# The closing part of a decoder block: gathered block, norm weight and last sums rearranged, with VectorE in program order

## The chip, the cores and the metric

The kernel runs on one core of a Trainium2 chip. The metric is the time of one execution on the device in microseconds (us). Three runs of the kernel before took 1557.12, 1559.18 and 1560.58 us; the median is 1559.18 us. In the rows PE is the matrix engine (PEld its weight loads), DVE the vector engine, ACT the scalar engine, POOL GpSimd, and SP the engine whose queue issues most transfers; a q behind a name (DVEq, SPq) is that engine's sequencer.

## What is computed

The reference is one decoder block over 512 tokens of width 1024: attention and gated linear attention side by side, then a channel mixer that retrieves experts, then a final norm. Only the mixer's end and the norm bear on the change:

```
def peer_ffn(h, wq, subkeys, u, v):      # per token: 8 heads x 16 of 16384 experts
    ...
    ub = jnp.take(u, eb, axis=0)
    hid = jax.nn.gelu(jnp.einsum('tkd,td->tk', ub, xb), approximate=False) * gb
    vb = jnp.take(v, eb, axis=0)
    return jnp.einsum('tk,tkd->td', hid, vb)

x = x + gate2 * peer_ffn(...)            # gate2: one row of 1024 for the sequence
y = x * rsqrt(mean(x * x) + 1e-6) * final_norm_w
```

The last two lines are the closing part: for each token the mixer's sum times gate2, plus the residual x, the norm over 1024 columns, and the product with the norm's weight.

## The kernel before

The 512 tokens are four blocks of 128. For three of them (DENSE, blocks 0 to 2, 384 tokens) the mixer isn't gathered: all 16,384 experts are run through as 128 chunks of 128. For chunk c, `u_part(c)` makes the hidden values (`ph`, 24 matmuls of 128x384) and `v_part(c)` scales them by the gates and splits them and the chunk's rows of v into a high and a low part (`Ah`, `Al`, `vc..h`, `vc..l`; the low parts are DVE's, lines 60 and 1029). `v_matmuls` adds the chunk's contribution to six PSUM accumulators `acc0` to `acc5` (block i, column half q: `acc[2*i+q]`): 3 matmuls of 128x512 (`mm3`, lines 64 to 66) for each accumulator, 18 for a chunk. The last four chunks (LAST = 4, c = 124 to 127) are held back and done block by block, first half 0, then half 1, so that block 0 is ready first.

The fourth block (GB = 3) is gathered. POOL issues 128 gathers of u rows (`gu`, line 887) and 128 of v rows (`gv`, line 897) into a ring of buffers; DVE multiplies each `gu` with `h2n` and sums it (line 889) and adds each `gv` to `gacc` (line 902). `gather_to`, line 1068, spreads them over 124 chunks.

At c = 112 the tile `h2n` is overwritten with gate2: DVE makes a diagonal tile `dg` (line 1074), PE multiplies it with ones (`g2b`, line 1079), ACT copies the result to `h2n` (line 1080). From there on `h2n` is the gate row.

`finish(n, ...)`, lines 1039 to 1059, closes a block: load x (line 1043), gate (1047), add x (1048), squares on ACT with a sum for each half (1049), their sum (1050), `rstd_of` (lines 70 to 82: mean, Ln and Exp on ACT, one Newton step on DVE in lines 78 to 81), then one instruction for each half that multiplies with the rstd and with the norm weight `fwb` (1058), and the store (1059). For block 1 the scale is ACT's (1055) and the weight POOL's (1056). Block 3 is finished ahead of the last four chunks' preparation, then blocks 0, 1, 2 as their accumulators end.

The order on each engine comes from a scheduler that simulates the program, except for POOL, which keeps the order of the code. On an engine the instructions start in their order; a waiting one holds back those behind it.

Of the kernel before, what the change touches and what calls it, by code (L numbers as in the profile page):

```python
# [17 lines left out]
P = 128  # L18
D = 1024
# [3 lines left out]
EPS = 1e-6  # L23
# [13 lines left out]
GR = 5  # L37
# [4 lines left out]
def peer_block_kernel(ctx: ExitStack, tc: tile.TileContext, a: dict, out: bass.AP):  # L42
    nc = tc.nc
# [3 lines left out]
    ps = ctx.enter_context(tc.tile_pool(name="ps", bufs=2, space=PSUM, side="left"))  # L47
# [60 lines left out]
    x1d = dr.tile([NT, P, D], F32, name="x1d")  # L108
# [14 lines left out]
    def pbank(name):  # L123
        return ps.tile([P, 512], F32, tag="ph", name=name)
# [46 lines left out]
    xf = frA.tile([P, 2, 32], F32, name="xf")  # L171
# [5 lines left out]
    for L in LW:  # L177
        m = 64 >> L
# [50 lines left out]
    for n in range(NT):  # L229
        sq = frA.tile([P, D], F32, tag="m4", bufs=2, name=f"sqa{n}")  # L230
        ss = frA.tile([P, 2], F32, tag="ss", bufs=2, name=f"ssa{n}")
# [3 lines left out]
        r = rstd_of(frA, ss[:, 0:1], float(D), 1, f"ra{n}")  # L235
# [376 lines left out]
    h2n = h2p.tile([P, D], F32, name="h2n")  # L612
# [74 lines left out]
    def u_part(c, lo_eng=None):  # L687

        j = c // 2 % 2
        if j == 0:  # L690
            u_part.raw[c % 2] = raw([P, 2, KD, P], f"u{c}")
            nc.sync.dma_start(u_part.raw[c % 2], a["uT"][c // 4 + (c % 2) * (P // 4)])
        uh, ul = hilo(u_part.raw[c % 2][:, j], [P, KD, P], f"uc{c}", lo_eng or nc.vector)
        ph = ps.tile([P, 512], F32, tag="ph", name=f"ph{c}")[:, :TD]
        for k in range(KD):
            mm3(ph, uh[:, k, :], ul[:, k, :], h2Th[:, k, :TD], h2Tl[:, k, :TD], k == 0, k == KD - 1)
        ge = dnA.tile([P, NGRP, TG], F32, tag="ge", bufs=RING, name=f"ge{c}")
        gef = ge.rearrange("p g t -> p (g t)")
# [226 lines left out]
    gp = ctx.enter_context(tc.tile_pool(name="gp", bufs=1, side="left", reuse_waits="tile"))  # L925
# [106 lines left out]
    def v_matmuls(parts, blocks=range(len(DENSE)), qs=(0, 1)):  # L1032
        for c, Ah, Al, vh, vl in parts:
            for i in blocks:
                for q in qs:
                    mm3(acc[2 * i + q], Ah[:, i * P:(i + 1) * P], Al[:, i * P:(i + 1) * P],
                        vh[:, q * 512:(q + 1) * 512], vl[:, q * 512:(q + 1) * 512], c == 0, c == P - 1)

    def finish(n, srcs, xr=None, pool=False):
        gate2b = h2n  # L1040
        y = gp.tile([P, D], F32, tag="gr", bufs=GR, name=f"y{n}")
        xr = xr if xr is not None else gp.tile([P, D], F32, tag="gr", bufs=GR, name=f"xf{n}")
        nc.sync.dma_start(xr, x1d[n])
        ss = dn.tile([P, 2], F32, tag="ss", bufs=2, name=f"ssf{n}")
        for q in range(2):
            qs = slice(q * 512, (q + 1) * 512)
            nc.vector.tensor_tensor(y[:, qs], srcs[q], gate2b[:, qs], OP.mult)
            nc.vector.tensor_tensor(y[:, qs], y[:, qs], xr[:, qs], OP.add)
            nc.scalar.activation(xr[:, qs], y[:, qs], AF.Square, accum_out=ss[:, q:q + 1])
        nc.vector.tensor_tensor(ss[:, 0:1], ss[:, 0:1], ss[:, 1:2], OP.add)  # L1050
        r = rstd_of(dn, ss[:, 0:1], float(D), 1, f"rf{n}")
        for q in range(2):
            qs = slice(q * 512, (q + 1) * 512)
            if pool:
                nc.scalar.activation(y[:, qs], y[:, qs], AF.Copy, scale=r)
                nc.gpsimd.tensor_tensor(y[:, qs], y[:, qs], fwb[:, qs], OP.mult)
            else:
                nc.vector.scalar_tensor_tensor(y[:, qs], y[:, qs], r, fwb[:, qs], op0=OP.mult, op1=OP.mult)
            nc.sync.dma_start(out[n * P:(n + 1) * P, qs], y[:, qs])

    LEAD = 8
    for c in range(1, 1 + LEAD, 2):
# [22 lines left out]
    for i in range(len(DENSE)):  # L1085
# [62 lines left out]
```

## Time and profile before

| | us |
|---|---|
| median of three runs | 1559.18 |
| the profiled execution | 1555.13 |
| its span, first to last instruction | 1553.4 |
| PE busy / share of the span | 1493.2 / 96% |
| DVE busy | 1251.8 / 81% |
| ACT busy | 688.8 / 44% |
| POOL busy | 412.9 / 27% |
| TensorE clock granted, mean | 0.99 of full speed |

The profiled execution is 1.7 us longer than its span, and 4.05 us shorter than the median. Busy shares are means over the whole span, and the closing part is its last 2%: there the stretch itself has to be read.

### The profile page before, as it was taken

Reading aid. Unit: us, or ns where it says so; the run is one execution under the profiler, and the core shown is the slowest. Engines: PE = TensorE matmul, PEld = TensorE weight load, DVE = VectorE, ACT = ScalarE, POOL = GpSimd, SP = SyncE. Lnnn points to the kernel's source line nnn. Section 1 sums busy time; section 2 is a strip of 40 time slices with the busy share of each in tenths; the row PEclk is TensorE's granted clock in tenths of the full one; section 3 lists DMA queues with packets and bytes.
Section 4 is the critical chain, followed back from the end, with each engine's and each line's share of the span. In section 5 each row is a group of like instructions: output and inputs, shape, how many; then the busy total and the mean of one; then the engine's idle time right before and its main releaser. Section 6 shows DMA issues by size and latency. Waiting matters only on the chain.

```text
span 1553.4 us, 24408 instructions
## 1 busy us (share of the span) xinstructions
PE 1493.2 (96%) x9379; PEld 1328.2 (86%) x9379; DVE 1251.8 (81%) x2476; ACT 688.8 (44%) x1078; POOL 412.9 (27%) x327
## 2 busy tenths in 40 slices
PE   4999989899999999999999999999999999999996
PEld 3787878888998999999888888888888888888885
DVE  7578668589989898995678778878888878887997
ACT  5545576433445666564333333333333333333343
POOL 1000000144500000003243334433434434434550
PEclk9999999999999999999999999999999999999998
DMA  9253444262346677679998999888998989898893
GB/s 349 89 204 131 171 142 173 108 239 92 127 155 188 198 239 235 201 239 388 380 348 317 339 348 346 322 340 333 364 330 329 338 340 354 326 340 334 292 331 129
DMA packets 154932, 409.67 MB, mean 264 GB/s; under 512 B 10288, under 2 KB 77120, under 8 KB 142400
## 3 DMA queue, kind: packets, MB, share of 16 engines
q1 hardware_dynamic: 108736, 261.30, 47.2%
q0 software_dynamic: 36864, 134.23, 23.0%
q10 hardware_dynamic: 9216, 12.59, 2.2%
q8 instruction: 73, 1.20, 0.3%
q14 instruction: 43, 0.35, 0.1%
HBM read 366.14 MB, written 41.94 MB: 263 GB/s over the span
## 4 chain that ended last, share of the span: by engine, by line
PE 63%; DVE 3%; DMA 2%; ACT 1%; issue 1%; DVEq 0%; ACTq 0%; SPq 0%
PE acc L65 11%; PE acc L64 11%; PE acc L66 11%; PE ph L66 8%; PE ph L64 8%; PE ph L65 8%; PE pg L874 4%; DMA Gd<-gs 1%; DMA gr<-Gd 1%; DVE o L867 1%; ACT gs L876 0%; DVE o L862 0%; DVE oh L819 0%; DVE oh L822 0%; DVE oh L817 0%
## 5 line engine op out<-in xcount | busy, mean ns | idle before, releaser
L887 POOL DMA_INDIRECT gu<-in_u_dram,ix_u x128 | 170.2, 1329 | 531.5 <-PE pg L874 273.5
L897 POOL DMA_INDIRECT gv<-in_vP_dram,ix_v x128 | 171.0, 1336 | 214.9 <-DVE gu L889 183.1
L902 DVE SCALAR_TENSOR_TENSOR gacc<-gv,hg,gacc 128x1024 f32<-128x1024 f32 x127 | 162.7, 1281 | 3.3 <-DMA gv<-in_vP_dram,ix_v 3.1
L889 DVE SCALAR_TENSOR_TENSOR gu<-gu,h2n 128x1024 f32<-128x1024 f32 x128 | 156.0, 1219 | 5.9 <-DMA gu<-in_u_dram,ix_u 5.9
L1028 ACT ACTIVATE Ah<-ge 128x384 fp32r<-128x384 f32 x64 | 33.6, 525 | 155.1 <-PE acc L65 155.1
L1028 ACT ACTIVATE Ah<-gel 128x384 fp32r<-128x384 f32 x64 | 33.6, 525 | 154.4 <-PE acc L65 154.4
L876 ACT ACTIVATE gs<-pg 128x512 f32<-128x512 f32 x96 | 94.3, 1108 | 9.8 <-PE pg L874 9.8
L867 DVE TENSOR_TENSOR o<-o,gp 128x1024 bf16<-128x1024 bf16 x144 | 91.0, 687 | 4.3
L874 PE MATMUL pg<-o,o 128*128 128x128 bf16 x1152 | 79.3, 223 | 5.3 <-DVE o L867 5.3
L874 PEld LDWEIGHTS <-o 128*128 128x128 bf16 x1152 | 69.7, 99 | 14.4 <-issue 8.5
L953 POOL IOTA iot<- 128x256 bf16 x1 | 1.5, 1541 | 282.8 <-DVE h2Tl L675 282.8
L1029 DVE TENSOR_TENSOR Al<-gel,Ah 128x384 fp32r<-128x384 f32 x64 | 35.6, 556 | 45.2 <-ACT Ah L1028 45.2
L699 ACT ACTIVATE ge<-ph 128x384 f32<-128x384 f32 x128 | 60.8, 475 | 23.8 <-PE ph L66 23.7
L862 DVE TENSOR_TENSOR o<-iot,t 128x2048 bf16<-128x2048 bf16 x48 | 58.5, 1218 | 4.9 <-ACT t L842 4.9
L1029 DVE TENSOR_TENSOR Al<-ge,Ah 128x384 fp32r<-128x384 f32 x64 | 35.5, 555 | 19.2 <-ACT Ah L1028 18.1
L1024 DVE TENSOR_TENSOR ge<-ge,gr 128x384 f32<-128x384 f32 x64 | 35.4, 553 | 10.9 <-ACT ge L699 10.9
L212 DVE SCALAR_TENSOR_TENSOR macc<-wa,scs,macc 128x1024 f32<-128x1024 f32 x28 | 39.0, 1392 | 4.9 <-DMA wa<-in_w_ada_dram 4.7
L1024 DVE TENSOR_TENSOR gel<-gel,gr 128x384 f32<-128x384 f32 x64 | 32.8, 553 | 0.0
L65 PE MATMUL pq<-h2Tl,wq_0h 128*128 128x512 f32 (+1 forms) x80 | 27.9, 349 | 1.2 <-DVE h2Tl L675 1.2
L64 PE MATMUL pq<-h2Th,wq_0h 128*128 128x512 f32 (+1 forms) x80 | 28.0, 352 | 1.0 <-ACT qha L751 1.0
L65 PE MATMUL pq<-h2Tl,wq_1h 128*128 128x512 f32 (+1 forms) x80 | 28.2, 353 | 0.0
L66 PE MATMUL pq<-h2Th,wq_1l 128*128 128x512 f32 (+1 forms) x80 | 28.2, 352 | 0.0
(2599 smaller groups left out, 5077.1 us busy)
## 6 DMA issues: line engine op xcount, KB each, us to landing
u<-in_uT_dram SPq DMA_DIRECT2D x64, 1024.0 KB
v<-in_vP_dram SPq DMA_DIRECT2D x64, 1024.0 KB
Gd<-gs SPq DMA_DIRECT2D x24, 1024.0 KB
gr<-Gd SPq DMA_DIRECT2D x16, 1536.0 KB
wa<-in_w_ada_dram SPq DMA_DIRECT2D x20, 1024.0 KB
gsp<-ge ACTq DMA_DIRECT2D x64, 192.0 KB
gel<-gsp SPq DMA_DIRECT2D x32, 384.0 KB
wi<-in_w_in_dram SPq DMA_DIRECT2D x9, 1024.0 KB
```

Source lines behind the costliest of these rows:

```text
L64: nc.tensor.matmul(acc, lh, rh, start=start, stop=False)
L65: nc.tensor.matmul(acc, lh, rl, start=False, stop=False)
L66: nc.tensor.matmul(acc, ll, rh, start=False, stop=stop)
L867: nc.vector.tensor_tensor(o2[:, :, m], o12[:, :, 1], gp3[:, g0:g0 + H, m, None].to_broadcast([P, H, P, 2]), OP.mult)
L874: nc.tensor.matmul(pt[:, i, :], o12[:, g, 0, :, r], o2[:, g, m, :, r], start=(m == 0), stop=(m == 2))
L876: nc.scalar.activation(gs[:, :, t0 + 4 * f:t0 + 4 * f + 4].rearrange("p b a -> p a b"), pt, AF.Copy)
L887: nc.gpsimd.indirect_dma_start(out=ur, out_offset=None, in_=a["u"], in_offset=bass.IndirectOffsetOnAxis(ap=ix_u[:, s:s + 1], axis=0))
L889: nc.vector.scalar_tensor_tensor(ur, ur, 1.0, h2n, op0=OP.mult, op1=OP.mult, accum_out=hid[:, s:s + 1])
L897: nc.gpsimd.indirect_dma_start(out=vr, out_offset=None, in_=a["vP"], in_offset=bass.IndirectOffsetOnAxis(ap=ix_v[:, s:s + 1], axis=0))
L902: nc.vector.scalar_tensor_tensor(gacc, vr, hg[:, s:s + 1], gacc, op0=OP.mult, op1=OP.add)
L1024: nc.vector.tensor_tensor(ge, ge, v_part.g[:, :, c % CG, :], OP.mult)
L1029: nc.vector.tensor_tensor(Al, gef, Ah, OP.subtract)
```

## The change

It rewrites `finish`. Block 3 gets a function of its own, `finish_gathered`, called after chunk 122: whole rows of 1024 columns, squares and mean in one DVE instruction, and the inverse root by DVE alone (`rsqrt_dve`: an integer start value and three Newton steps of three instructions). The gathers are spread over 122 chunks instead of 124. Blocks 0 to 2 use a class `Finish`: gate and add (`gated`), squares on ACT (`squared`), the product with the norm weight as DVE instructions of their own (`weighed`), which stand beside ACT's Ln and Exp, then the Newton step, and the final scale by ACT or DVE (`close`). Block 2's half 1 is closed before the last four chunks: `acc5` ends at chunk 123 and is gated and added at once, and the last four chunks' part of it goes to two new accumulators of 256 columns, `pl512` and `pl768`. Its output leaves in three pieces of 320, 384 and 320 columns. From `fs = [...]` on DVE keeps the order of the code.

```diff
                 for q in qs:
+                    end = P - LAST if (i, q) == (len(DENSE) - 1, 1) else P
                     mm3(acc[2 * i + q], ..., c == 0, c == end - 1)
-    def finish(n, srcs, xr=None, pool=False):
...
+    def rsqrt_dve(pool, m, name):
+        nc.vector.tensor_scalar(y.bitcast(I32), m.bitcast(I32), -0.5, 1597463007.0, op0=OP.mult, op1=OP.add)
+        for _ in range(3):
+            nc.vector.scalar_tensor_tensor(t, y, y, m, op0=OP.mult, op1=OP.mult)
+            nc.vector.tensor_scalar(t, t, -0.5, 1.5, op0=OP.mult, op1=OP.add)
+            nc.vector.tensor_tensor(y, y, t, OP.mult)
+    def finish_gathered():
+        nc.sync.dma_start(xr, x1d[GB])
+        nc.vector.tensor_tensor(y, gacc, h2n, OP.mult)
+        nc.vector.tensor_tensor(y, y, xr, OP.add)
+        nc.vector.scalar_tensor_tensor(xr, y, 1.0 / D, y, op0=OP.mult, op1=OP.mult, accum_out=ss)
+        nc.vector.tensor_scalar(ss, ss, EPS, None, op0=OP.add)
+        r = rsqrt_dve(dn, ss, "r3")
+        nc.vector.scalar_tensor_tensor(y, y, r, fwb, op0=OP.mult, op1=OP.mult)
+        nc.sync.dma_start(out[GB * P:(GB + 1) * P, :], y)
+    class Finish:
+        def gated(self, cs, src):
+            nc.vector.tensor_tensor(self.y[:, cs], src, h2n[:, cs], OP.mult)
+            nc.vector.tensor_tensor(self.y[:, cs], self.y[:, cs], self.xr[:, cs], OP.add)
+        def squared(self, cs):
+            nc.scalar.activation(xr[:, cs], y[:, cs], AF.Square, scale=1.0 / 32.0, accum_out=self.ss[:, j:j + 1])
+            if j == 1:
+                nc.vector.tensor_scalar(self.ss[:, 3:4], self.ss[:, 0:1], self.ss[:, 1:2], EPS, op0=OP.add, op1=OP.add)
+        def weighed(self, *css):
+                nc.vector.tensor_tensor(self.y[:, cs], self.y[:, cs], fwb[:, cs], OP.mult)
+        def close(self, rest, parts):
+            if len(self.ps) == 3:
+                nc.vector.tensor_tensor(m, m, ss[:, 2:3], OP.add)
+            nc.scalar.activation(r, m, AF.Ln)
+            nc.scalar.activation(r, r, AF.Exp, scale=-0.5)
+            self.weighed(*rest)
+            nc.vector.scalar_tensor_tensor(t, r, r, m, op0=OP.mult, op1=OP.mult)
+            nc.vector.tensor_scalar(t, t, -0.5, 1.5, op0=OP.mult, op1=OP.add)
+            nc.vector.tensor_tensor(r, r, t, OP.mult)
+            for on_act, cs in parts:
+                if on_act:
+                    nc.scalar.activation(y[:, cs], y[:, cs], AF.Copy, scale=r)
+                else:
+                    nc.vector.tensor_scalar(y[:, cs], y[:, cs], r, None, op0=OP.mult)
+                nc.sync.dma_start(out[n * P:(n + 1) * P, cs], y[:, cs])
-        gather_to(EARLY + (len(gathers) - EARLY) * (c + 1) // (P - LAST))
+        gather_to(EARLY + (len(gathers) - EARLY) * (c + 1) // (P - LAST - 2))
+        if c == P - LAST - 2:
+            finish_gathered()
-    finish(GB, [gacc[:, 0:512], gacc[:, 512:1024]])
...
+    ctx.enter_context(tc.manual_schedule(engines={mybir.EngineType.DVE}))
+    fs = [Finish(n, xl[:, i - 1, :] if i else x0) for i, n in enumerate(DENSE)]
+    fs[-1].gated(half[1], acc[-1])
+    for i, f in enumerate(fs):
         v_matmuls(last, (i,), (0,))
-        v_matmuls(last, (i,), (1,))
-        finish(DENSE[i], [acc[2 * i], acc[2 * i + 1]], xl[:, i - 1, :] if i else None, pool=(i == 1))
+        f.gated(half[0], acc[2 * i])
+        f.squared(half[0])
+        if i + 1 < len(DENSE):
+            v_matmuls(last, (i,), (1,))
+            f.gated(half[1], acc[2 * i + 1])
+            f.squared(half[1])
+            f.close(half, [(True, h) for h in half])
+        else:
+            quarter = [slice(512, 768), slice(768, 1024)]
+            for cs, done in zip(quarter, (half[0], quarter[0])):
+                pl = ps.tile([P, 512], F32, tag="ph", name=f"pl{cs.start}")[:, :256]
+                for c, Ah, Al, vh, vl in last:
+                    mm3(pl, ..., vh[:, cs], vl[:, cs], c == P - LAST, c == P - 1)
+                nc.vector.tensor_tensor(f.xr[:, cs], pl, h2n[:, cs], OP.mult)
+                nc.vector.tensor_tensor(f.y[:, cs], f.y[:, cs], f.xr[:, cs], OP.add)
+                f.squared(cs)
+                f.weighed(done)
+            f.close(quarter[1:], [(False, slice(0, 320)), (True, slice(640, 1024)), (False, slice(320, 640))])
```

**DVE, the closing of blocks 0 to 2.** A name's number behind the underscore is the buffer's. Before, with the scheduler's order, from block 2's first add of x to its second:

```order
L1048 TENSOR_TENSOR y2_14835<-y2_14835,xl_14711 128x512
L1050 TENSOR_TENSOR ssf1_14787<-ssf1_14787 128x1
L78 TENSOR_TENSOR rf0t_14749<-rf0y_14748 128x1
L75 TENSOR_SCALAR rf1m_14795<-ssf1_14787 128x1
L79 TENSOR_TENSOR rf0t_14749<-rf0t_14749,rf0m_14747 128x1
L80 TENSOR_SCALAR rf0t_14749<-rf0t_14749 128x1
L81 TENSOR_TENSOR rf0y_14748<-rf0y_14748,rf0t_14749 128x1
L1047 TENSOR_TENSOR y2_14835<-acc5_8211,h2n_2430 128x512
L1058 SCALAR_TENSOR_TENSOR y0_14736<-y0_14736,rf0y_14748,fwb_8212 128x512 x2
L78 TENSOR_TENSOR rf1t_14797<-rf1y_14796 128x1
L1048 TENSOR_TENSOR y2_14835<-y2_14835,xl_14711 128x512
```

With the change, on the same engine, the end of block 1 and the start of block 2:

```order
L1077 TENSOR_TENSOR y1_14715<-y1_14715,xl_14708 128x512
L1084 TENSOR_SCALAR ssf1_14716<-ssf1_14716 128x1
L1089 TENSOR_TENSOR y1_14715<-y1_14715,fwb_8212 128x512 x2
L1100 SCALAR_TENSOR_TENSOR tf1_14799<-rf1_14798,ssf1_14716 128x1
L1101 TENSOR_SCALAR tf1_14799<-tf1_14799 128x1
L1102 TENSOR_TENSOR rf1_14798<-rf1_14798,tf1_14799 128x1
L1076 TENSOR_TENSOR y2_14718<-acc4_8210,h2n_2430 128x512
L1077 TENSOR_TENSOR y2_14718<-y2_14718,xl_14708 128x512
L1158 TENSOR_TENSOR xl_14708<-pl512_14826,h2n_2430 128x256
L1159 TENSOR_TENSOR y2_14718<-y2_14718,xl_14708 128x256
L1084 TENSOR_SCALAR ssf2_14719<-ssf2_14719 128x1
L1089 TENSOR_TENSOR y2_14718<-y2_14718,fwb_8212 128x512
```

Before, the blocks' steps lie in between each other; now a block's steps stand together, and block 2's gate of `acc4` stands behind all of block 1's.

**DVE, while the last four chunks are prepared.** Before, ahead of the last low part, `vc127l`:

```order
L60 TENSOR_TENSOR vc126l_14694<-v126_14691,vc126h_14693 128x1024
L1050 TENSOR_TENSOR ssf3_14647<-ssf3_14647 128x1
L75 TENSOR_SCALAR rf3m_14655<-ssf3_14647 128x1
L78 TENSOR_TENSOR rf3t_14657<-rf3y_14656 128x1
L79 TENSOR_TENSOR rf3t_14657<-rf3t_14657,rf3m_14655 128x1
L1029 TENSOR_TENSOR Al127_14708<-ge127_14433,Ah127_14707 128x384
L80 TENSOR_SCALAR rf3t_14657<-rf3t_14657 128x1
L81 TENSOR_TENSOR rf3y_14656<-rf3y_14656,rf3t_14657 128x1
L1058 SCALAR_TENSOR_TENSOR y3_14644<-y3_14644,rf3y_14656,fwb_8212 128x512 x2
L60 TENSOR_TENSOR vc127l_14703<-v126_14691,vc127h_14702 128x1024
```

With the change:

```order
L60 TENSOR_TENSOR vc126l_14691<-v126_14688,vc126h_14690 128x1024
L1061 TENSOR_SCALAR ss3_14619<-ss3_14619 128x1
L1045 TENSOR_SCALAR r3g_14624<-ss3_14619 128x1
L1076 TENSOR_TENSOR y2_14718<-acc5_8211,h2n_2430 128x512
L1047 SCALAR_TENSOR_TENSOR r3n_14625<-r3g_14624,ss3_14619 128x1
L1029 TENSOR_TENSOR Al127_14705<-ge127_14442,Ah127_14704 128x384
L1077 TENSOR_TENSOR y2_14718<-y2_14718,xl_14708 128x512
L1048 TENSOR_SCALAR r3n_14625<-r3n_14625 128x1
L60 TENSOR_TENSOR vc127l_14700<-v126_14688,vc127h_14699 128x1024
```

Block 3's last product moved behind `vc127l`, and block 2's early gate and its add of x (`xl`, loaded late) moved ahead of it.

**ACT, the copies of gate2 into `h2n`.** Before:

```order
L59 ACTIVATE vc115h_14266<-v114_14231 128x1024
L1080 ACTIVATE h2n_2430<-g2b0_14155 128x512
L1080 ACTIVATE h2n_2430<-g2b1_14161 128x512
L1028 ACTIVATE Ah117_14376<-ge117_13910 128x384
L59 ACTIVATE uc125h_14303<-u125_14301 128x1024
L59 ACTIVATE vc116h_14336<-v116_14334 128x1024
```

With the change:

```order
L1028 ACTIVATE Ah117_14385<-ge117_13919 128x384
L59 ACTIVATE uc125h_14312<-u125_14310 128x1024
L1028 ACTIVATE Ah118_14451<-gel116_14349 128x384
L59 ACTIVATE vc116h_14345<-v116_14343 128x1024
L1129 ACTIVATE h2n_2430<-g2b0_14164 128x512
L1129 ACTIVATE h2n_2430<-g2b1_14170 128x512
```

The copies moved four instructions down, because three more gathers stand ahead of c = 112's overwrite, the last of them `gu126` instead of `gu124`, which still reads the old `h2n`; on PE the `g2b` matmuls move from ahead of chunk 113 to the middle of chunk 114, and the 24 matmuls of `ph123` from the start of chunk 114 to the middle of chunk 116. Up to c = 112 the order on every engine is that of before.

## Rows read from the trace of the kernel before

**Rows 1.** Windows: us; busy PE, PEld, DVE, ACT, POOL (count); clock, DMA share, GB/s

```profile
1450.00:1500.00 50.00, 50.00 (x251) 44.27 (x250) 46.43 (x58) 17.53 (x26) 31.05 (x22) 1.00 0.87 303
...
1534.00:1541.60 7.60, 7.58 (x34) 5.88 (x32) 6.93 (x18) 4.21 (x14) 0.00 (x0) 1.00 0.00 0
1541.60:1553.40 11.80, 0.00 (x0) 0.00 (x0) 6.68 (x16) 2.24 (x6) 2.49 (x2) 0.58 0.35 133
```

**Rows 2.** Chain of waits from PE's end to the last instruction: start us, us, what

```profile
1541.62 0.69 DVE y L1047
1542.31 1.32 DVE y L1058 x2
...
1545.06 1.23 ACT y L1055 x2
...
1546.64 0.40 DVE rf2t L78
...
1547.07 1.20 DVE rf2t L79
...
1548.48 0.17 DVE rf2y L81
...
1548.67 0.75 DVE y L1058
```

**Rows 3.** DVE's timeline from 1526 us: start, duration, line, operation, [idle before, releaser]

```profile
1528.20 1.22 DVE L60 TENSOR_TENSOR vc127l<-v,vc127h 128x1024 fp32r<-128x1024 f32 x1
1534.06 1.29 DVE L1047 TENSOR_TENSOR y<-acc,h2n 128x512 f32<-128x512 f32 x2 [4.65 <-PE acc L66]
...
1545.09 0.16 DVE L1050 TENSOR_TENSOR ssf<-ssf 128x1 f32<-128x1 f32 x1 [0.34 <-ACT xl L1049]
```

**Rows 4.** Timelines of ACT and of POOL after PE's end, columns as in group 3

```profile
1544.34 0.63 ACT L1049 ACTIVATE xl<-y 128x512 f32<-128x512 f32 x1 [2.90 <-DVE y L1048]
...
1546.19 0.18 ACT L76 ACTIVATE rf2y<-rf2m 128x1 f32<-128x1 f32 x1
1545.75 2.49 POOL L1056 TENSOR_TENSOR y<-y,fwb 128x512 f32<-128x512 f32 x2 [36.54 <-ACT y L1055]
```

**Rows 5.** The store's line: count, duration in ns min/median/max, first and last start

```profile
L1059 SPq DMA_DIRECT2D out_dram<-y x8: 332/332/338, 1527.6 to 1550.1; - x8
```

**Rows 6.** Single lines elsewhere, like the new instructions: ns min/median/max, first and last start

```profile
L451 DVE TENSOR_TENSOR Eg<-Eg,gq x14: 415/419/427, 82.4 to 139.3; 128x256 f32<-128x256 f32 x14
L406 DVE TENSOR_SCALAR sS<-sS,Z x32: 281/348/354, 114.7 to 202.4; 128x256 f32<-128x256 f32 x24, 128x128 f32<-128x128 f32 x8
L348 ACT ACTIVATE Eg<-pn x8: 376/381/399, 165.0 to 210.1; 128x256 f32<-128x256 f32 x8
```

**Rows 7.** PE's timeline, neighbouring matmuls of 256 and of 512 columns

```profile
278.48 0.28 PE L64 MATMUL pq<-h2Th,wq_1h 128*128 128x256 f32 x1
278.60 0.28 PE L65 MATMUL pq<-h2Tl,wq_1h 128*128 128x256 f32 x1
...
1539.36 0.39 PE L64 MATMUL acc<-vc125h,Ah 128*128 128x512 f32 x1
1539.59 0.39 PE L65 MATMUL acc<-vc125l,Ah 128*128 128x512 f32 x1
```

**Rows 8.** Late inputs: SP's timeline, two windows, uses of two tiles, DVE's timeline

```profile
1522.05 0.81 SPq L1043 DMA_DIRECT2D xl<-x1d  x2
...
1525.00:1526.00 1.00, 1.00 (x6) 0.83 (x5) 0.42 (x3) 0.84 (x4) 0.00 (x0) 1.00 0.95 389
1526.00:1527.00 1.00, 1.00 (x7) 0.80 (x6) 0.92 (x4) 0.93 (x1) 0.00 (x0) 1.00 0.02 4
...
L65 PE MATMUL acc<-vc127l,Ah x6: 388/394/394, 1533.4 to 1541.0; 128*128 128x512 f32 x6
...
L65 PE MATMUL acc<-vc117l,Ah x6: 394/394/394, 1492.1 to 1495.6; 128*128 128x512 f32 x6
...
1484.31 1.23 DVE L60 TENSOR_TENSOR vc117l<-v,vc117h 128x1024 fp32r<-128x1024 f32 x1
```

More of the change, by code (lines that the diff above doesn't have):

```diff
@@ L1035, in v_matmuls @@
                 for q in qs:
+                    end = P - LAST if (i, q) == (len(DENSE) - 1, 1) else P
                     mm3(acc[2 * i + q], Ah[:, i * P:(i + 1) * P], Al[:, i * P:(i + 1) * P],
-                        vh[:, q * 512:(q + 1) * 512], vl[:, q * 512:(q + 1) * 512], c == 0, c == P - 1)
-    def finish(n, srcs, xr=None, pool=False):
[L1040 to L1059, printed above, removed]
@@ new lines, in v_matmuls @@
+                        vh[:, q * 512:(q + 1) * 512], vl[:, q * 512:(q + 1) * 512], c == 0, c == end - 1)
+    def rsqrt_dve(pool, m, name):
+        y = pool.tile([P, 1], F32, name=name + "g", tag="rsg", bufs=1)
+        t = pool.tile([P, 1], F32, name=name + "n", tag="rsn", bufs=1)
+        nc.vector.tensor_scalar(y.bitcast(I32), m.bitcast(I32), -0.5, 1597463007.0, op0=OP.mult, op1=OP.add)
[3 more added lines that the diff above has]
+            nc.vector.tensor_tensor(y, y, t, OP.mult)
+        return y
@@ new lines, in finish_gathered @@
+    def finish_gathered():
+        y = gp.tile([P, D], F32, tag="gr", bufs=GR, name="y3")
+        xr = gp.tile([P, D], F32, tag="gr", bufs=GR, name="xf3")
+        nc.sync.dma_start(xr, x1d[GB])
+        ss = dn.tile([P, 1], F32, name="ss3")
+        nc.vector.tensor_tensor(y, gacc, h2n, OP.mult)
[5 more added lines that the diff above has]
+        nc.sync.dma_start(out[GB * P:(GB + 1) * P, :], y)
@@ new lines, in peer_block_kernel, with __init__ @@
+    class Finish:
+        def __init__(self, n, xr):
+            self.n, self.xr, self.ps = n, xr, []
+            self.y = gp.tile([P, D], F32, tag="gr", bufs=GR, name=f"y{n}")
+            self.ss = dn.tile([P, 4], F32, tag="ss", bufs=3, name=f"ssf{n}")
+            nc.sync.dma_start(xr, x1d[n])
+        def gated(self, cs, src):
+            nc.vector.tensor_tensor(self.y[:, cs], src, h2n[:, cs], OP.mult)
+            nc.vector.tensor_tensor(self.y[:, cs], self.y[:, cs], self.xr[:, cs], OP.add)
+        def squared(self, cs):
+            j, y, xr = len(self.ps), self.y, self.xr
+            nc.scalar.activation(xr[:, cs], y[:, cs], AF.Square, scale=1.0 / 32.0, accum_out=self.ss[:, j:j + 1])
+            if j == 1:
+                nc.vector.tensor_scalar(self.ss[:, 3:4], self.ss[:, 0:1], self.ss[:, 1:2], EPS, op0=OP.add, op1=OP.add)
+            self.ps.append(cs)
+        def weighed(self, *css):
+            for cs in css:
+                nc.vector.tensor_tensor(self.y[:, cs], self.y[:, cs], fwb[:, cs], OP.mult)
+        def close(self, rest, parts):
+            n, y, ss, m = self.n, self.y, self.ss, self.ss[:, 3:4]
+            if len(self.ps) == 3:
+                nc.vector.tensor_tensor(m, m, ss[:, 2:3], OP.add)
+            r = dn.tile([P, 1], F32, tag="rsy", bufs=3, name=f"rf{n}")
+            t = dn.tile([P, 1], F32, tag="rst", bufs=3, name=f"tf{n}")
+            nc.scalar.activation(r, m, AF.Ln)
[10 more added lines that the diff above has]
+                nc.sync.dma_start(out[n * P:(n + 1) * P, cs], y[:, cs])
@@ L1080, in peer_block_kernel @@
                 nc.scalar.activation(h2n[:, q * 512:(q + 1) * 512], pb, AF.Copy)
+        if c == P - LAST - 2:
+            finish_gathered()
     tc.keep_in_program_order(nc.scalar.preload_act_table_set("natural_log_exp_and_others"))
-    finish(GB, [gacc[:, 0:512], gacc[:, 512:1024]])
     last = [v_part(c) for c in range(P - LAST, P)]
     xl = dn.tile([P, 2, D], F32, tag="vraw", bufs=2, name="xl")
-    for i in range(len(DENSE)):
-        v_matmuls(last, (i,), (0,))
-        v_matmuls(last, (i,), (1,))
-        finish(DENSE[i], [acc[2 * i], acc[2 * i + 1]], xl[:, i - 1, :] if i else None, pool=(i == 1))
+    x0 = gp.tile([P, D], F32, tag="gr", bufs=GR, name="xf0")
+    half = [slice(0, 512), slice(512, 1024)]
+    ctx.enter_context(tc.manual_schedule(engines={mybir.EngineType.DVE}))
+    fs = [Finish(n, xl[:, i - 1, :] if i else x0) for i, n in enumerate(DENSE)]
+    fs[-1].gated(half[1], acc[-1])
+    for i, f in enumerate(fs):
+        v_matmuls(last, (i,), (0,))
+        f.gated(half[0], acc[2 * i])
[10 more added lines that the diff above has]
+                for c, Ah, Al, vh, vl in last:
+                    mm3(pl, Ah[:, i * P:(i + 1) * P], Al[:, i * P:(i + 1) * P], vh[:, cs], vl[:, cs],
+                        c == P - LAST, c == P - 1)
+                nc.vector.tensor_tensor(f.xr[:, cs], pl, h2n[:, cs], OP.mult)
[3 more added lines that the diff above has]
+            f.close(quarter[1:], [(False, slice(0, 320)), (True, slice(640, 1024)), (False, slice(320, 640))])
 def layouts(inp):
```

## The prediction

> **What bounds the kernel now.** I read the windows first. In the steady part PE is busy 50.00 of 50 us [rows 1], up to its last matmul at about 1541.6 us; DVE is the next, 46.43 of 50, so it follows PE with little to spare. After 1541.6 PE does nothing: 11.8 us remain, in which DVE works 6.68, ACT 2.24 and POOL 2.49 us [rows 1]. The change can gain only there, or lose by making PE wait earlier. So the second view is the chain of waits through this tail [rows 2], and the third the timelines that show what stands in front of what [rows 3, 4]. The reader is to see that block 2's closing has three foreign things in it. DVE does block 0's two products of line 1058 (1.32 us) between block 2's gate and its add. ACT does block 1's two scales of line 1055 (1.23 us) before block 2's Ln. And two Newton steps of one column take 0.40 and 1.20 us while POOL runs block 1's weight products (2.49 us from 1545.75) [rows 4]; the next ones, with POOL done, are 0.19 apart (1548.48 to 1548.67). The last store is issued at 1550.1 [rows 5] and the span ends 3.3 us later. The execution has 1.7 us more than the span.
>
> **What is removed.** All three go. The first: 1.32 us of line 1058 plus 0.07 of a Newton step that stood in the way, about 1.4. The second: L1050 begins 0.75 after the last square starts (1544.34 to 1545.09), so without the scales Ln would start at about 1545.45 instead of 1546.19 [rows 3, 4], 0.75. The third: (0.40 - 0.19) + (1.20 - 0.19) = 1.2. Together 3.4 us, if nothing else took their place.
>
> **What is added on PE.** `acc5`'s twelve matmuls of 512 columns become 24 of 256. Neighbours of 512 start 0.23 apart, of 256 0.12 [rows 7]: 24 x 0.12 - 12 x 0.229 = +0.13 us. PE would end at 1541.7, and `pl512` at about 1540.3.
>
> **What is added on DVE: program order.** This decides. Each block now runs as one piece on DVE: gate, add, gate, add, mean, two weight products, three Newton steps. Take 512 columns at 0.69 each when the next step needs the result (I add 0.03 for the hand-over, as in the 0.19 of the 0.16 us steps), and 0.60 when it doesn't (two gates in 1.29, so the second starts 0.60 after the first) [rows 3]. From the gate's start: add 0.72; second gate 1.32; second add 2.04; ACT's square 2.76; the mean, 0.75 behind it, 3.51; two weight products at 3.59 and 4.19; Newton at 4.79, 4.98, 5.17. ACT's Ln and Exp take 0.45 (1546.19 to 1546.64) [rows 4] and hide under the two products. The next block's gate starts at 5.25. In each block DVE stands 0.8 us still for the squares, and nothing of the next block may fill it.
>
> The first gate waits for `acc0`. It was 1534.06 [rows 3]; in the new order PE ends `acc0` three matmuls earlier (3 x 0.23), so about 1533.4. Block 1's gate then comes at 1538.6 and block 2's at 1543.9. But `acc4`, which block 2's first gate reads, is done before 1540, and all of PE's work at 1541.7. So PE no longer sets the end: DVE is 2 us behind it.
>
> Block 2, from 1543.87: gate, add at +0.72, quarter `pl512` at +1.32 (a 256-column product is 0.42 [rows 6]), its add +1.77, ACT's square at +2.22 (0.38 [rows 6] and a read), mean +2.74, weight product of half 0 +2.82, quarter `pl768` +3.42, its add +3.87, a quarter's weight product +4.2, ACT's square of the last quarter +4.32 to +4.82, sum +4.84, last weight product +4.91, Ln and Exp +5.02 to +5.45, Newton +5.48, +5.67 and +5.86, final scale +6.05. Two scales of 320 columns on DVE, estimated at 0.38 from 0.348 at 256 columns [rows 6], run beside one of 384 on ACT, estimated at 0.5 from 0.38 at 256. They end at +6.7, 1550.6. Three stores of 0.33 each [rows 5] are issued from +6.46 on; the third at 1551.05, 0.95 after before's last one. The pieces are smaller than before's 256 KB, which I take as up to 0.1 us. So the tail is 0.85 us longer: 3.4 gained, 4.3 given back by 4.9 us of DVE work and stalls that now lie behind each other. (POOL's two products and line 1058's pairs of blocks 0 and 2 go; six weight products of DVE come, and four scales on ACT and the three in the end.)
>
> Bounds: if a dependent step needs no more than the independent 0.60, each of the six dependent steps of 512 columns saves 0.12 and the end is 0.1 later instead of 0.85. If the squares' answer takes 1.0 us instead of 0.75, three stalls add 0.75, and the end is 1.6 later. The final scales have their cover (each runs beside another); if ACT's 384 columns took 0.7, as 512 do, nothing changes, since the last DVE scale ends later.
>
> The Trainium skill, "VectorE: DVE Perf Modes", section "Rules for kernel authors", says of chained DVE ops to minimise their count, since each pays its drain whatever semaphores lie between. This case's rows show no such cost as long as the next step is independent (0.60 apart at a duration of 0.69). By the page, the six products would be added whole (6 x 0.69 = 4.1 instead of 3.6), and the end would be 0.5 us later still.
>
> **What moves earlier.** (a) Block 3's finish: three Newton rounds instead of one (nine steps of 0.19) and a final product that goes behind `vc127l`; four instructions of 512 become two of 1024. DVE had 4.65 us of idle time after `vc127l` [rows 3], and 1.3 us of product moving there is covered. (b) Block 2's early gate and add stand ahead of `vc127l`: 2 x 0.65 us, minus the product that left (1.4). So `vc127l` starts at about 1527.9, as before (1528.20). PE first uses it at 1533.4 [rows 8], in the new order some 0.7 us earlier; it is ready at 1529.1. Cover 3.5 us, so nothing. The add needs `xl`, issued at 1522.05 and landed by 1526 (the DMA share is 0.95 up to 1526.00 and 0.02 after it) [rows 8]; DVE gets there at about 1527.2. Behind it stand `vc127l` and so PE. (c) The `h2n` copies, `g2b` and `ph123` go later by half a chunk to two chunks. PE has the same matmuls to do in another order. What it needs next is ready long before: `vc117l`, behind the copies, starts at 1484.31 and is used at 1492.1 [rows 8], 6.6 us after it ends. The copies now wait for two more gathers; as long as these land within that cover it costs nothing, which I take. The bounds are 0 and the excess over 6.6 us, for which no row gives a size; it goes to rival 2.
> (d) Gathers: POOL goes through its list in its own order and its instructions stay in the same sequence, so 122 instead of 124 moves only the `h2n` overwrite, (c).
>
> **Rivals.** 1, faster: DVE keeps up with PE. That needs the dependent steps and the squares' answer to be much cheaper than the rows say. The chain after PE's end would then be quarter, add, square, sum, Newton, scale, store: 0.45 + 0.45 + 0.52 + 0.6 + 0.6 + 0.4 + 3.3 = 6.3 us behind 1541.7, plus a store's 0.7: span 1548.8, 4.6 us less. For it to count, 2 of DVE's 10.5 us before block 2 have to go. The 0.12 us of dependent steps are six times 0.12 = 0.7; so not, from these rows. It would give 1554.6 us.
> 2, slower: the add of `xl` comes too early. If `xl` lands after 1530.7, `vc127l` ends after PE's need of it at 1532.7 and PE loses a us for each us. It decides from there: landing at 1534 costs 3.3 us and gives 1563.4 us. Against: the landing at 1526 [rows 8] and the same place of the issue, behind `vc125l`. A loss of the same size could come at (c).
> 3, the split doesn't do what it says: the 256-column matmuls are paced by their weights. A weight load takes 0.19 us; at that pace the 24 take 4.5 us, 1.8 more on PE. But DVE reads `pl768` only at 1547.3, and PE would end at 1543.5: hidden, and the forecast stands. Rows 7 speak against it too.
>
> **How the numbers follow.** The profiled execution would be 1555.13 + 0.85 = 1556.0. Before's was 4.05 us under the median, so against the median of 1559.18 I forecast 1560.0 us, no change that can be told. About 0.2%, 3.1 us, is what a measurement of this kernel can tell from no change: its three runs lie 3.5 us apart. Forecast 0.86, rival 1 0.05, rival 2 (with (c)) 0.09; rival 3 has 0.1 within the forecast. The range reaches from the forecast with its lower bound and the runs' own spread, 1559.3 - 3.3 = 1556.0, to the upper bound and the spread, 1560.8 + 2.2 = 1563.0. Of the forecast's 0.86, 0.84 stays within 0.2%, 0.01 falls on each side: faster 0.06, same 0.84, slower 0.10.
>
> **What would show it.** In the tail of the changed trace: block 0's gate at 1533.4, block 1's 5.25 us later, block 2's 10.5; DVE's idle time before the mean of each block about 0.8, released by ACT; the chain after 1541.7 on DVE alone, with no wait on PE; Newton steps 0.19 apart; no POOL; last store at 1551.0. It is wrong if `vc127l` or a low part near chunk 117 shows up as PE's releaser, or if block 2's gates wait for PE.

## The result, and the profile after

The changed kernel took 1568.24 us (median of six runs, 1564.87 to 1579.43) against 1557.07 us for the kernel before (six runs, 1554.99 to 1560.58). The ratio is 1.0077, with a 95% interval of 1.0049 to 1.0105: 11 us slower. The forecast was 1560.0 us and no change, with a range up to 1563.0. The profiled execution took 1569.58 us, its span is 1567.8 us.

First the windows of the changed kernel, as in [rows 1]: the steady part, and the stretch from PE's last matmul to the end. Columns: window, its length; busy us (and instructions) of PE, PEld, DVE, ACT, POOL; clock, DMA share, GB/s.

```profile
800.00:1400.00 600.00, 600.00 (x2865) 520.71 (x2864) 482.07 (x623) 210.56 (x297) 248.62 (x185) 1.00 0.90 333
...
1554.65:1567.80 13.15, 0.01 (x1) 0.00 (x0) 7.53 (x22) 5.08 (x15) 0.00 (x0) 0.62 0.23 86
```

PE ends at 1554.66, 13.1 us later than before, and the tail behind it is 13.1 us long instead of 11.8. So the tail has 1.3 us of the loss, and the rest was lost before PE's end, where the forecast put 0.13 us. Not all of PE's 13.1 us belongs to the change. The last sums' first matmul, of chunk 0, started 3.4 us later already, before:

```profile
764.58 1.65 PE L64 MATMUL acc<-vc0h,Ah 128*128 128x512 f32 x6 [1.52 <-ACT vc0h L59]
```

and with the change:

```profile
767.96 1.43 PE L64 MATMUL acc<-vc0h,Ah 128*128 128x512 f32 x5 [1.52 <-ACT vc0h L59]
```

Up to there both kernels do the same in the same order, and the traces of kernels that are alike up to there begin chunk 0 anywhere from 763.9 to 769.3 us; what sets that was not followed. The other 9.7 us lie between this matmul and PE's end (777.0 us before, 786.7 with the change). Yet PE waits nowhere in the steady part: it is busy 600.00 of 600 us at full clock, as before. It only does less in that time. The same window of the kernel before:

```profile
800.00:1400.00 600.00, 600.00 (x2901) 528.76 (x2900) 487.42 (x630) 213.30 (x301) 244.40 (x188) 1.00 0.90 339
```

2901 matmuls before, 2865 with the change, in a stretch in which the order on all engines is the same. The busy share can't show this: a matmul that starts later after its neighbour counts as busy all the same. The timelines of PE do. In their rows, `acc<-vc60h,Ah` names the moving operand first (512 columns of `vc60h`) and then the stationary one (128 columns of `Ah`, which PEld loads). The first and the last of the 18 matmuls of chunk 60 of the last sums, before:

```profile
1138.04 0.39 PE L64 MATMUL acc<-vc60h,Ah 128*128 128x512 f32 x1
...
1141.94 0.39 PE L66 MATMUL acc<-vc60h,Al 128*128 128x512 f32 x1
```

and with the change:

```profile
1145.98 0.39 PE L64 MATMUL acc<-vc60h,Ah 128*128 128x512 f32 x1
...
1149.95 0.39 PE L66 MATMUL acc<-vc60h,Al 128*128 128x512 f32 x1
```

Seventeen steps in 3.90 us before, 0.2294 each; in 3.97 us with the change, 0.2335. Over the 32 chunks between 900 and 1100 us the means, from the start times in ns, are 0.22907 and 0.23334. The 384-column matmuls of the first sums kept their distance (0.1744 and 0.1741). There are 2304 matmuls of 512 columns before the change, so 2304 x 0.00427 = 9.8 us. With the tail's 1.3 that makes 11.1; the medians differ by 11.2.

The tail itself went as forecast. DVE's timeline of the changed kernel (start, duration, line, operation, idle time before and its releaser), which answers to [rows 3]:

```profile
1546.37 0.69 DVE L1076 TENSOR_TENSOR y<-acc,h2n 128x512 f32<-128x512 f32 x1 [2.65 <-PE acc L66]
1547.09 0.69 DVE L1077 TENSOR_TENSOR y<-y,xf 128x512 f32<-128x512 f32 x1
...
1549.90 0.22 DVE L1084 TENSOR_SCALAR ssf<-ssf 128x1 f32<-128x1 f32 x1 [0.79 <-ACT xf L1082]
...
1551.75 0.68 DVE L1076 TENSOR_TENSOR y<-acc,h2n 128x512 f32<-128x512 f32 x1
...
1555.28 0.21 DVE L1084 TENSOR_SCALAR ssf<-ssf 128x1 f32<-128x1 f32 x1 [0.79 <-ACT xl L1082]
...
1557.12 0.68 DVE L1076 TENSOR_TENSOR y<-acc,h2n 128x512 f32<-128x512 f32 x1
...
1563.38 0.68 DVE L1107 TENSOR_SCALAR y<-y,rf 128x320 f32<-128x320 f32 x2
```

The blocks' gates stand 5.38 and 5.37 us apart (forecast 5.25), DVE stands still 0.79 us for the squares of block 0 and of block 1 (0.8), and from block 2's gate to its final scales it is 6.26 us (6.05). DVE doesn't wait for PE in block 2 at all.

### The profile page after: what moved, and what is told of

The parts are those of the page before. It is cut to its first block, busy times and chain, and to the rows that moved or that the text cites. A ratio compares the mean times of both kernels' runs of the same rounds, so it can differ in the third digit from the quotient of the medians.

```text
span 1567.8 us, 24441 instructions
## 1 busy us (share of the span) xinstructions
PE 1504.0 (96%) x9391; PEld 1327.7 (85%) x9391; DVE 1256.4 (80%) x2484; ACT 688.8 (44%) x1077; POOL 415.4 (26%) x325
## 4 chain that ended last, share of the span: by engine, by line
PE 62%; DVE 4%; DMA 2%; ACT 1%; issue 1%; SPq 0%; DVEq 0%; ACTq 0%
PE acc L65 11%; PE acc L66 11%; PE acc L64 11%; PE ph L66 8%; PE ph L64 8%; PE ph L65 8%; PE pg L874 4%; DMA Gd<-gs 1%; DMA v<-in_vP_dram 1%; DVE o L867 0%; ACT gs L876 0%; DVE o L862 0%; DVE oh L819 0%; DVE oh L822 0%; DVE oh L817 0%
## 5 line engine op out<-in xcount | busy, mean ns | idle before, releaser
L887 POOL DMA_INDIRECT gu<-in_u_dram,ix_u x128 | 174.6, 1364 | 529.5 <-DVE o L867 270.0
```

The lines of the kernel that those rows point to most:

```text
L887: nc.gpsimd.indirect_dma_start(out=ur, out_offset=None, in_=a["u"], in_offset=bass.IndirectOffsetOnAxis(ap=ix_u[:, s:s + 1], axis=0))
```

## The experiments

What could make the same matmuls, in the same order, start farther apart? The instructions of the loop are the same, but not the places of their tiles in SBUF. The change adds small tiles to the pool that also holds `fwb`, `gacc`, the ring of gates, `Ah`, `Al` and the raw v tiles. The pool ends at a fixed place on the right, and each small tile takes 32 bytes of a partition; four more of them move all the rest 128 bytes down. Read from the two built kernels, in bytes of a partition, with the rest modulo 512:

```
                                 before           with the change
Ah (chunk 60), stationary    200416   224         200288    96
Al (chunk 60), stationary    206560   224         206432    96
raw v (chunk 60)             220896   224         220768    96
gacc                         171744   224         171616    96
vc60h, moving                 91936   288          91936   288
h2Th, moving in first sums    48416   288          48416   288
```

The number behind each address is that rest; it is called the place of a tile from here on. All buffers of `Ah` and `Al` and their blocks of 128 columns lie multiples of 512 bytes apart, so one rest holds for all. Theory A: these places set the pace. Theory B: the loss comes from what the change does to the order around c = 112 and in the closing part.

**The places alone, and the change with before's places.** Kernel e1 is the kernel before with four unused buffers:

```diff
-        ss = dn.tile([P, 2], F32, tag="ss", bufs=2, name=f"ssf{n}")
+        ss = dn.tile([P, 2], F32, tag="ss", bufs=6, name=f"ssf{n}")
```

> The kernel before, with nothing changed but four more 8-byte tiles (32 bytes each) in the pool that holds gacc, the gate ring, Ah, Al and the raw v tiles: the pool grows by 128 bytes at its right end and all of these start 128 bytes lower, as they do with the change. The instructions and their order are those of before. Theory A (the place of these tiles in SBUF sets the pace of the 512-column matmuls): neighbours 0.2333 us apart instead of 0.2289, 2304 of them, so 10 us more: 1567. Theory B (the order of work around c = 112, the gathers' pace or the closing part does it): as before, 1557.

Kernel e2 is the changed kernel with its small tiles in shared buffers and 32 bytes of padding:

```diff
-        y = pool.tile([P, 1], F32, name=name + "g", tag="rsg", bufs=1)
-        t = pool.tile([P, 1], F32, name=name + "n", tag="rsn", bufs=1)
+        y = pool.tile([P, 1], F32, name=name + "g", tag="rsy", bufs=2)
+        t = pool.tile([P, 1], F32, name=name + "n", tag="rst", bufs=2)
-        ss = dn.tile([P, 1], F32, name="ss3")
+        ss = dn.tile([P, 4], F32, tag="ss", bufs=3, name="ss3")[:, 0:1]
-            r = dn.tile([P, 1], F32, tag="rsy", bufs=3, name=f"rf{n}")
-            t = dn.tile([P, 1], F32, tag="rst", bufs=3, name=f"tf{n}")
+            r = dn.tile([P, 1], F32, tag="rsy", bufs=2, name=f"rf{n}")
+            t = dn.tile([P, 1], F32, tag="rst", bufs=2, name=f"tf{n}")
+    dn.tile([P, 8], F32, name="pad")
```

> The changed kernel, with its small tiles sharing buffers and a pad of 32 bytes, so that gacc, the gate ring, Ah, Al and the raw v tiles start where they do before. Theory A: the 512-column matmuls are 0.229 apart again and only the tail's cost is left: 1557 + 0.85 to 1.5, so 1558 to 1559. Theory B: 1568, as the changed kernel.

e1 took 1567.22 us against 1557.12, ratio 1.0057 (1.0039 to 1.0075). e2 took 1558.18, ratio 1.0000 (0.9989 to 1.0010). The steady windows, e1:

```profile
800.00:1400.00 600.00, 600.00 (x2865) 520.74 (x2864) 482.01 (x621) 210.56 (x297) 243.47 (x185) 1.00 0.90 333
```

and e2:

```profile
800.00:1400.00 600.00, 600.00 (x2901) 528.83 (x2901) 488.52 (x633) 213.90 (x302) 244.62 (x188) 1.00 0.91 338
```

2865 and 2901: each kernel has the count that goes with its places, not with its code. Theory B falls: as built, e1 has before's instructions in before's order on every engine, and e2 the change's. What the change does to the work costs 1 us (1558.18 against 1557.12), not told from nothing; four small tiles cost 10.

**Which tile.** The pad of 128 bytes was put at two places inside the pool, in the kernel before. e3 has it between `Al` and the raw v tiles, e4 between the ring of gates and `Ah`:

```diff
         Al = dn.tile([P, TD], FR, tag="Al", bufs=4, name=f"Al{c}")
+        if c == 0:                                   # e3
+            dn.tile([P, 32], F32, name="pad")
...
             v_part.g = dn.tile([P, NGRP, CG, TG], F32, tag="gring", bufs=2, name=f"gr{c}")
+            if c == 0:                               # e4
+                dn.tile([P, 32], F32, name="pad")
```

> The kernel before with a pad of 128 bytes between Al and the raw v tiles: gacc, the gate ring, Ah and Al start 128 bytes lower, the raw v tiles where they were. If the place of the stationary operands Ah and Al counts: 0.2333 between 512-column matmuls, 1567. If the place of the raw v tiles does (DMA writes them, ACT and DVE read them): 0.2289, 1557.

> The kernel before with the pad of 128 bytes between the gate ring and Ah: only fwb, gacc and the gate ring start 128 bytes lower, Ah, Al and the raw v tiles where they were. If the place of Ah and Al counts: 0.2289, 1557. If that of gacc or the gate ring does (DVE's gathers and products run beside every matmul): 0.2333, 1567.

One run each: e3 1569.65 us, e4 1554.85. The windows, e3:

```profile
800.00:1400.00 600.00, 600.00 (x2865) 520.75 (x2864) 482.08 (x622) 210.97 (x298) 243.87 (x185) 1.00 0.90 333
```

and e4:

```profile
800.00:1400.00 600.00, 600.00 (x2900) 528.70 (x2899) 487.13 (x630) 213.65 (x302) 244.02 (x187) 1.00 0.91 338
```

In e4 `fwb`, `gacc` and the gates moved and nothing happened. In e3 `Ah` and `Al` moved too, the raw v tiles did not, and the whole loss is there. So it is the place of the stationary operands of the last sums.

**Which places.** Each of the four buffers of `Ah` and `Al` got a place of its own, so that one run shows four:

```diff
-        Ah = dn.tile([P, TD], FR, tag="Ah", bufs=4, name=f"Ah{c}")
-        Al = dn.tile([P, TD], FR, tag="Al", bufs=4, name=f"Al{c}")
+        o = (72, 88, 104, 120)[c % 4]                # p1: 0, 64, 128, 192; p2: (80, 112, 0, 16)
+        Ah = dn.tile([P, TD + 128], FR, tag=f"Ah{c % 4}", bufs=1, name=f"Ah{c}")[:, o:o + TD]
+        Al = dn.tile([P, TD + 128], FR, tag=f"Al{c % 4}", bufs=1, name=f"Al{c}")[:, o:o + TD]
```

> A measurement, the kernel before with each of the four Ah and Al buffers at a place of its own: a chunk's stationary operands start at byte 0, 64, 128 or 192 of a 512-byte row of SBUF (c modulo 4), where before has 224 and the change 96 for all. Read is the distance of neighbouring 512-column matmuls of each chunk. If the place within 256 or 512 bytes sets the pace, the four chunks differ, between 0.225 and 0.235 us; if it is something else that moved with the pool, they are alike.

> The same with 32, 160, 224 and 288: 224 is before's own place and should be 0.229 us again; 32 and 288 tell whether the row counts by 256 or by 512 bytes (alike if by 256).

The 512-byte row is a way of giving the place modulo 512; nothing here shows such rows in SBUF. In p1 (1567.66 us in its one run) all four are slow: 0.2333, 0.2330, 0.2341 and 0.2329 us for 0, 64, 128 and 192 (seven or eight chunks each). In p2 (1557.49) they differ: 0.2291 for 32, 0.2328 for 160, 0.2291 for 224 and 0.2267 for 288. So 32 and 288 seem not to be alike; "Using it" shows why they are. Two chunks of p2, at 288 and at 160, first and last matmul (3.85 and 3.96 us for 17 steps):

```profile
1006.89 0.39 PE L64 MATMUL acc<-vc39h,Ah 128*128 128x512 f32 x1
...
1010.74 0.39 PE L66 MATMUL acc<-vc39h,Al 128*128 128x512 f32 x1
...
1019.28 0.40 PE L64 MATMUL acc<-vc41h,Ah 128*128 128x512 f32 x1
...
1023.24 0.40 PE L66 MATMUL acc<-vc41h,Al 128*128 128x512 f32 x1
```

The moving operands lie at 288 throughout, so the best place seems to be the moving operand's own. p3 left `Ah` and `Al` at 224 and moved the others, by multiples of 32 bytes that differ from chunk to chunk:

```diff
+            c = int(name[2:])
+            o = (c % 4 if name[0] == "v" else c // 2 % 4) * 8
+            hi = pool.tile([P, D + 32], FR, tag="hi", bufs=bufs, name=name + "h")[:, o:o + D]
+            lo = pool.tile([P, D + 32], FR, tag="lo", bufs=bufs, name=name + "l")[:, o:o + D]
```

> The kernel before with the moving operands of the last sums (vh, vl) and the stationary ones of the first (uh, ul) at places that differ from chunk to chunk by multiples of 32 bytes; Ah and Al stay at 224. If only the stationary operand's place counts, the 512-column matmuls stay at 0.229 us in all chunks while the 384-column ones (0.174 before) vary with uh, ul; if the moving one's does, the 512-column ones vary.

Both: the 512-column distances are 0.2318 to 0.2337 in every chunk, with `Ah` and `Al` at the place that is good in the kernel before, and the 384-column ones run from 0.1738 (`uh` at 288, where their moving operand `h2Th` lies) to 0.1766 (at 256 and 448). It took 1579.91 us in its one run; 14 us of that lie ahead of the last sums (chunk 0 starts at 778.73 us), and were not followed. The place of either operand counts, so it may be the difference. p4 varies both, for 128 pairs:

```diff
+            o = int(name[2:]) * 5 % 7 * 8            # moving, in tiles of D + 48 columns
...
+        o = c * 11 % 16 * 8                          # stationary, in tiles of TD + 128 columns
```

> A measurement: in the kernel before, every chunk gets its own places, by multiples of 32 bytes, for the moving operands (vh, vl) and for the stationary ones (Ah, Al), 128 pairs in one run, and the first sums' stationary ones (uh, ul) vary as well. From the runs so far I expect the distance of neighbouring 512-column matmuls to depend on the difference of the two places modulo 256: 0.2265 to 0.229 us at differences of 0 and 64, 0.232 to 0.2335 elsewhere. The rival is that each operand has good places of its own (224, 32, 288 for the stationary, 288 for the moving): then pairs with difference 0 away from these are slow.

108 chunks of the steady part, by the difference of the places of moving and stationary operand modulo 256; the mean over a chunk's neighbours of 512 columns, worked out from the timeline:

```
difference (bytes)   chunks   mean us   lowest to highest
   0                   16     0.2283    0.2265 to 0.2335
  32                   16     0.2331    0.2324 to 0.2335
  64                    7     0.2307    0.2288 to 0.2335
  96                    7     0.2332    0.2329 to 0.2335
 128                   16     0.2321    0.2318 to 0.2329
 160                   16     0.2341    0.2335 to 0.2347
 192                   15     0.2332    0.2329 to 0.2335
 224                   15     0.2330    0.2324 to 0.2335
```

Sorted by the stationary operand's place alone, the means of its eight places are 0.2316 to 0.2330; by the moving one's alone 0.2318 to 0.2326. Neither has good places of its own; the difference sorts them. At 0, 15 of 16 chunks have at most 0.2294, whatever the two places are. Before has the difference 64, the change 192; p3's differences are 32, 96, 128 and 192, none of them a good one. At 160 the matmuls are slower than I expected (0.2341). The one slow chunk at 0 is chunk 113, and only its first step is long, behind the 16 `g2b` matmuls of c = 112 (0.31 us to the next):

```profile
1484.00 0.48 PE L71 MATMUL acc<-vc113h,Ah 128*128 128x512 f32 x1
1484.31 0.39 PE L72 MATMUL acc<-vc113l,Ah 128*128 128x512 f32 x1
```

In all 16 chunks the last eight of the 17 steps take 0.2266 to 0.2268. Left open is 64: in five of its seven chunks these steps take 0.2285 to 0.2293, in two 0.2334. Both of the two have the moving operand at 96 and the stationary one at 32 modulo 256, which none of the five has. (p4 took 1573.14 us in its one run.)

**Using it.** e6 is the kernel before with 448 bytes of padding between `Al` and the raw v tiles, which puts `Ah` and `Al` at 288:

```diff
         Al = dn.tile([P, TD], FR, tag="Al", bufs=4, name=f"Al{c}")
+        if c == 0:
+            dn.tile([P, 112], F32, name="pad448")
```

> The kernel before with a pad of 448 bytes between Al and the raw v tiles, so that Ah and Al start at 288 of a 512-byte row, where their moving operands vh and vl start, instead of 224. If the difference counts: 0.2265 instead of 0.2289 us between 512-column matmuls, 2304 of them, 5 us less: 1552. If 224 was already as good as any place: 1557.

1555.25 us against 1557.17, ratio 0.9986 (0.9973 to 1.0000). The mean distance is 0.2278, not 0.2265: chunks at 0.2291 and 0.2267 alternate. The window:

```profile
800.00:1400.00 600.00, 600.00 (x2912) 530.37 (x2911) 489.21 (x634) 215.08 (x304) 246.90 (x189) 1.00 0.91 339
```

2304 x (0.2291 - 0.2278) = 3 us by the distances, 2 us by the medians, not 5: I had taken the better of two kinds of chunk for all. The timing alone can hardly tell the gain from none (the interval reaches 1.0000); the distances can.

The timeline shows what the two kinds are. The slower ones are the even chunks, which stand right behind 24 matmuls of 384 columns. Chunk 58's first four and last three matmuls, and the first of chunk 59:

```profile
1126.32 0.39 PE L64 MATMUL acc<-vc58h,Ah 128*128 128x512 f32 x1
1126.55 0.40 PE L65 MATMUL acc<-vc58l,Ah 128*128 128x512 f32 x1
1126.78 0.40 PE L66 MATMUL acc<-vc58h,Al 128*128 128x512 f32 x1
1127.01 0.39 PE L64 MATMUL acc<-vc58h,Ah 128*128 128x512 f32 x1
...
1129.76 0.39 PE L64 MATMUL acc<-vc58h,Ah 128*128 128x512 f32 x1
1129.98 0.39 PE L65 MATMUL acc<-vc58l,Ah 128*128 128x512 f32 x1
1130.21 0.39 PE L66 MATMUL acc<-vc58h,Al 128*128 128x512 f32 x1
1130.44 0.39 PE L64 MATMUL acc<-vc59h,Ah 128*128 128x512 f32 x1
```

In the even chunks the first nine steps take 0.2312 us on average and the last eight 0.2267, as all of the odd ones do. The same holds in p2 for the chunks at 32, which are even: their last eight steps take 0.2267, like those at 288. So 32 and 288 are alike, and the place counts by 256 bytes. Why the start is slow was not tried.

**The tail.** e5 is e2 (so, before's places) without DVE's program order:

```diff
-    ctx.enter_context(tc.manual_schedule(engines={mybir.EngineType.DVE}))
```

> The changed kernel with before's places (as e2) and without DVE's program order: the scheduler places the closing of blocks 0 to 2. If program order is what took the 3.4 us of the tail back, DVE works ahead on blocks 1 and 2 while ACT squares: from block 0's gate about 14 us of DVE work to the end instead of 17.2, so 2 to 3 us less than e2: 1555 to 1556. If it is the added DVE work (six weight products), the same as e2: 1558.

1555.83 us against 1557.24, ratio 0.9991 (0.9976 to 1.0006); the timing can't tell it from the kernel before, the traces can. From PE's end to the span's end, e2:

```profile
1543.79:1556.90 13.11, 0.00 (x0) 0.00 (x0) 7.52 (x22) 5.08 (x15) 0.00 (x0) 0.70 0.23 86
```

and e5:

```profile
1543.29:1553.80 10.51, 0.00 (x0) 0.00 (x0) 5.17 (x21) 5.29 (x15) 0.00 (x0) 0.64 0.40 150
```

13.1 and 10.5 us, with 7.5 and 5.2 us of DVE work behind PE's end; the instructions of the two kernels are the same. So program order took 2.6 us, and without it the change's tail is 1.3 us shorter than before's 11.8. What is left to see in e5's chain of waits (start, us, what) is ACT's two scales of block 1 ahead of block 2's Ln:

```profile
1546.61 0.49 ACT xl L1082 x2
1547.10 1.22 ACT y L1105 x2
1548.33 0.10 ACT rf L1097
```

e7 is e5 with the padding of e6, and e8 is e7 with block 1's scales on DVE:

```diff
-            f.close(half, [(True, h) for h in half])
+            f.close(half, [(i == 0, h) for h in half])
```

> The version that the runs so far point to: the change without DVE's program order (e5) and with Ah and Al at 288 as in e6. The tail's 1.3 us and the matmuls' 5 us add: 1557 - 6.5 = 1550.5. If the place isn't what counts in e6: 1555.5, as e5.

> e7 with block 1's two final scales on DVE instead of ACT. In e5's tail ACT did them for 1.2 us ahead of block 2's Ln while DVE then stood still for 1.06 us. If that wait is the tail's last foreign piece, the Ln starts about 1 us earlier and the tail is 0.5 to 0.8 us shorter than e5's, the scales filling DVE's idle time; whole time about 1553.5 against e7's 1554.2, too little for the timing and to be read in the trace. If DVE's scales only get in the way of block 2's sum and last product: the tail is as long as before or longer.

e7 took 1554.24 us against 1557.17, ratio 0.9979 (0.9966 to 0.9992), e8 1553.48 against 1556.74, ratio 0.9973 (0.9960 to 0.9987): both beat the kernel before by 3 us, and the change by more. e7's forecast was 3.7 us too low: the padding's gain is 2 us, as in e6. e8's tail:

```profile
1540.91:1551.00 10.09, 0.00 (x0) 0.00 (x0) 5.97 (x23) 4.17 (x13) 0.00 (x0) 0.60 0.42 156
```

10.1 us against e5's 10.5, 0.4 less where 0.5 to 0.8 was expected. Its chain shows where the rest went, the two scales on DVE stand ahead of block 2's last sum:

```profile
1544.45 0.88 DVE y L1109 x2
1545.34 0.08 DVE ssf L1096
...
1545.44 0.21 ACT rf L1099
```

## Why the prediction was wrong

The step that failed is "What is added on PE". It took 0.229 us for all 512-column matmuls that the change leaves alone, because their order doesn't change, and added 0.13 us for the 24 new ones. The order was the same, as I had said; the tiles' places were not, and the 512-column matmuls of the whole loop ran at 0.2333. This term was missing: 2304 x 0.00427 = 9.8 us. e2 shows that it is the only large one: with before's places the change took 1558.18 us, inside the range. The sentence that shut the term out stands at the start: "The change can gain only there, or lose by making PE wait earlier." None of the rivals held it, since all of them asked where PE would wait, and PE waits no more than before. The added tiles were in the diff (`ss3`, `rsg`, `rsn`, and three buffers instead of two), and the places could have been read from the two built kernels ahead of the result. I had read a distance that belongs to one placing of the tiles as the price of the instruction.

The other steps:

- The tail by DVE's program order: right in its mechanism and nearly in size. Forecast 0.85 us more, measured 1.3 (e2's and the change's 13.1 against 11.8). What was too small are the one-column instructions that take a scalar from a tile instead of a constant: 0.21 us (L1084 above, L1100 alike) where I took 0.16, two on each block's path, 0.3 of the missing 0.45 us. The upper bound (1.6) holds.
- The three foreign pieces of 3.4 us: gone, as said. e5 shows that they are worth something once DVE may work ahead.
- The Trainium skill, "VectorE: DVE Perf Modes", section "Rules for kernel authors", puts a drain on every chained DVE op, by which the tail would have been some 1.35 us longer (0.85 + 0.5). That number is nearer to the measured 1.3 than mine, but by luck: the trace doesn't agree for independent ops, whose products stand 0.60 apart again (two weight products in 1.28 us), and what I missed lies for the most part in the one-column steps.
- What moves earlier: `vc127l` started at 1539.84 and was first used at 1545.7, 4.6 us after it ended (forecast 3.5); `vc117l` 8.4 us after it ended. The `h2n` copies, the early gate and the wait for `xl` cost nothing. Rival 2 did not occur; the time was on its side for another reason.
- Rival 3: the 256-column matmuls at 0.12 us, not paced by their weights.

In the range: bounds were put on every wait and every moved instruction, none on the pace of the work that stayed. The 3.3 and 2.2 us for the runs' own spread don't follow from the three runs, which lie 2.1 us under and 1.4 over their median; with these the range would have been narrower still.

## What to carry to other kernels

When PE is never idle, compare the number of matmuls in the same window of two traces, not the busy share: a loss of 1.9% a matmul was invisible in every idle time and every wait. A change that adds or resizes a tile moves other tiles of its pool; compare the places of the operands of the innermost matmuls before and after, and keep them with padding, before the change itself is judged. And where an engine is put into program order, add up what it can no longer do ahead: here 2.6 us in the last 13.

## What the runs showed of the hardware that I had not expected

The distance between neighbouring fp32r matmuls (K = 128, 128 stationary columns, 512 moving ones, a weight load for each) depends on where the two operands start in SBUF, by their difference modulo 256 bytes: 0.2283 us on average at 0, 0.2321 to 0.2341 at 32, 96, 128, 160, 192 and 224, and 0.2307 at 64 (p4). At 0 it was 0.2267 in the last eight of every chunk's 17 steps. With 384 moving columns it went from 0.1738 to 0.1766 in p3. There the differences sort otherwise: in p4 0.1743 at 0, 0.1733 at 64 and 0.1765 at 96. It isn't the clock: the granted clock was 1.00 in all these windows. What in the chip makes it so was not tried.
